# Four modulation chunks moved into the last step of a recurrent mixer, and half of an output product for four token tiles taken from raw weights

## The chip, the cores and the metric

The kernel runs on one core of a Trainium2 chip. The metric is the device time of one execution in microseconds. Engines are named as in the profile: PE is TensorE, DVE is VectorE, ACT is ScalarE, POOL is GpSimd, and SP is the queue that issues nearly all transfers.

## The reference, cut to what matters

The network has two layers for 512 latent tokens and 256 context tokens of width 1024. Only the first mixer of layer 0, a bidirectional gated recurrence, and the modulation vectors are touched.

```
m  = silu(c) @ ada_w + ada_b                     # 6 vectors of 1024 for each layer
u  = conv(px[..., D_RNN:]);  px = h @ w_in       # D_RNN = 1280 = 10 blocks of 128
a, b = coeffs(u, w_a, w_x, lambda)               # two gates per block and direction
hs = scan_forward(a, b) + scan_backward(a, b)
yx = (gelu(px[..., :D_RNN]) * hs) @ w_out        # the output product
x  = x + gt1 * yx
```

The modulation vectors of layer 1 (shift and scale of its first norm) are read only some 600 us after the stretch in which they are made here.

## The kernel before, in words

**The mixer's steps.** The ten blocks are worked in five pairs by `step(s)`, s = 0 to 5. Step s projects pair s (`stage_a`) and finishes pair s-1: the gates (`gates`, PE products into PSUM tiles `pg`, L623), the gated GELU branch (`stage_c`, PE products into `pa`, L415 and L416, and a GELU on ACT, L666), and the scans on DVE (`scans`). Step 5, the last, has no projection. For each of its two blocks and two directions ACT computes `tr`, `ti`, `q`, `a` (L631 to L638), DVE combines them (L640, L641, L643), and ACT turns `a` into the decay (L642). We call this sequence a gate group; there are four of them in the step, c0 forward, c0 backward, c1 forward, c1 backward. After the fourth come four square roots on ACT (L648), the last two GELUs, and the last scans, whose product with the GELU (L663) completes rows of `yrg`, the mixer's output y, transposed. The tiles `ti`, `q` and `a` have one buffer each, so a gate group of step 5 waits until the scans of step 4 have read theirs.

**The modulation chunks.** `ada(l, n)` makes 256 columns of a modulation vector: a 1 MB load into the pool `ws` (3 buffers, shared with `w_in` and `w_out`), 16 PE products (L176) into a `pg` tile, a copy to `part` on ACT (L178), and for every second chunk four small PE products (L185) into another `pg` tile and one or two additions on DVE (L188, L192). `pg` has two buffers, shared with the gates. There are 24 chunks, five in a step and four in step 4.

**The output product.** `mix_out` multiplies y (10 chunks of 128 rows) with `w_out` in two halves of 512 columns, for six token tiles. The rule is three PE products of split operands for each chunk: high times high, high times low, low times high (L808), where weights are split by ACT (`wohi`, L306) and POOL (`wolo`, L309), and y by ACT and DVE (`yt` for chunks 0 to 7, `yb` for 8 and 9). For the first half and the first four token tiles, chunks listed in `early` use the unsplit fp32 operands in one product (L804). `NEARLY[0]` is the number of such chunks. The first four tiles accumulate in PSUM tiles `po`, the other two in `pt`.

**What sets the order.** Outside regions marked as manual, the build step schedules each engine's queue from the code by costs of its own. Step 5 is manual for ACT alone, so ACT runs it as written there, and the other engines' order comes from that scheduler. Each engine then works its queue strictly in that order. The tiles of `mix_out` lie in memory that the mixer frees: `yt` and the routing tables wait for the last product of `stage_c`, the split weights for the last scans.

Of the kernel before, what the change touches and what calls it, by code (L numbers as in the profile page):

```python
# [17 lines left out]
P = 128  # L18
# [19 lines left out]
NPAIR = NE // 2  # L38
NWIDE = 6
FIRST = 5  # L40
NEARLY = 6, 4
KWB = 5
BIG = 1.0e30

# [58 lines left out]
class Net:  # L103
# [285 lines left out]
    def rg_mixer(self, ctx_y, wsp):  # L389
        tc, nc, A = self.tc, self.nc, self.A  # L390
        self.y = ctx_y.tile([P, NB, NTOK], F32, name="yrg")
        with ExitStack() as st:
# [35 lines left out]
            with tc.tile_pool(name="n0", bufs=1) as wk, tc.tile_pool(name="p0", bufs=2, space=PSUM) as p0:  # L428
# [18 lines left out]
                with tc.manual_schedule(engines={ET.PE, ET.DVE, ET.Activation, ET.Pool}):  # L447
# [7 lines left out]
                    rows = {}  # L455
# [93 lines left out]
                    parts = [split(uw[0], c, nc.gpsimd if c else nc.vector, wk, c) for c in range(2)]  # L549
# [34 lines left out]
            pb = st.enter_context(tc.tile_pool(name="pb", bufs=2, space=PSUM))  # L584
            ada = [(0, n) for n in range(8, 24)] + [(1, n) for n in range(8)]
            with tc.tile_pool(name="ma", bufs=2) as wa, tc.tile_pool(name="m0", bufs=2) as wk, \
# [27 lines left out]
                def gates(s, parts, c):  # L614
                    b = 2 * s + c
                    u = uc[b]
                    uh, ul, gh, gl = parts

                    def gate(m):
                        ps = pb.tile([P, 1024], F32, name="pg")  # L620
                        for j, (g, v) in enumerate(((gh, uh), (gh, ul), (gl, uh))):
                            for o, z in ((CTX, NTOK), (0, CTX)):
                                nc.tensor.matmul(ps[:, 256 + o:256 + z], g[:, m, :], v[:, o:z],  # L623
                                                 start=j == 0, stop=j == 2)
                        return ps[:, 256:1024]

                    for d in range(2):
                        v = d * NB + b
                        ps = gate(2 * d)
                        tr = wk.tile([P, NTOK], F32, name="tr", bufs=1)  # L630
                        nc.scalar.activation(tr, ps, AF.Tanh, scale=0.5, bias=self.ba[:, v:v + 1])  # L631
                        ps = gate(2 * d + 1)
                        ti = w1.tile([P, NTOK], F32, name=f"ti{2 * c + d}")
                        nc.scalar.activation(ti, ps, AF.Tanh, scale=0.5, bias=self.bx[:, v:v + 1])
                        q = w1.tile([P, NTOK], F32, name=f"q{2 * c + d}")
                        nc.scalar.activation(q, tr, AF.Exp, scale=self.cl[:, 0, v:v + 1], bias=self.cl[:, 0, v:v + 1])
                        a = w1.tile([P, NTOK], F32, name=f"a{2 * c + d}")
                        nc.scalar.activation(a, tr, AF.Tanh, scale=self.cl[:, 1, v:v + 1], bias=self.cl[:, 1, v:v + 1])  # L638

                        nc.vector.scalar_tensor_tensor(a, q, 1.0, a, op0=OP.add, op1=OP.mult)  # L640
                        nc.vector.scalar_tensor_tensor(q, a, 2.0, a, op0=OP.add, op1=OP.mult)  # L641
                        nc.scalar.activation(a, a, AF.Identity, bias=self.ones)  # L642
                        nc.vector.scalar_tensor_tensor(ti, ti, 1.0, u, op0=OP.add, op1=OP.mult)  # L643
                        yield c, d, q, a, ti
# [31 lines left out]
                NS = NB // 2  # L676
                wg = {}

                def step(s):
                    ps = []  # L680
                    if s < NS:
                        wg[s] = load_gates(s)
                        stage_a(s, uw[s])
                    if s >= 1:
                        wc = load(256 * (s - 1))
                        gp = [gate_parts(s - 1, wg[s - 1], c) for c in range(2)]
                        for c in range(2):
                            ps += gates(s - 1, gp[c], c)
                        if s == NS:
                            roots(ps)  # L690
                        for c in range(2):
                            stage_c(s - 1, wc, c)
                    if 0 < s < NS - 1:
                        uw.append(load(DR + 256 * (s + 1)))
                    for l, n in ada[s * 5:s * 5 + 5]:
                        self.ada(l, n, wsp, pb, wk)
                    if s >= 1:
                        if s < NS:
                            roots(ps)
                        scans(s - 1, ps)  # L700
# [6 lines left out]
    def mix_out(self, l, x, NT, y, K, W, rt, wsp, ypool, ytp, ring, nring):  # L707


        tc, nc, A = self.tc, self.nc, self.A  # L710
        V = nc.vector
# [4 lines left out]
        with ExitStack() as st:  # L716
# [5 lines left out]
            order = list(range(K)) if l == 0 else [0, 2, 4, 6, 1, 3, 5, 7]  # L722
# [9 lines left out]
            def parts(h, raw, i, ks):  # L732
                hi = wop.tile([P, 2, 512], F32R, name="wohi")
                lo = wop.tile([P, 2, 512], F32R, name="wolo")
                self.split(hi, lo, raw[:, ks, :], V if l and h == 0 and i else nc.gpsimd)
                for j, k in enumerate(range(4)[ks]):
                    wo[h, i + k] = hi[:, j, :], lo[:, j, :]
# [3 lines left out]
            if K > 8:  # L741
                yb = w1.tile([P, 2, K - 8, NT * P], F32R, name="yb")

            def rows(t, ks):
                self.split(yt[t][:, 0, ks], yt[t][:, 1, ks], y[:, ks, t * P:(t + 1) * P], V)

            raws = {i: load(0, i) for i in range(0, K, 4)}
            early = {k: (y[:, k, :], raws[k - k % 4][:, k % 4, :]) for k in order[0:NEARLY[l]]}
            if l == 0:
                parts(0, raws[4], 4, slice(2, 4))  # L750
                parts(0, raws[8], 8, slice(0, 2))
                for t in range(4):
                    rows(t, slice(6, 8))
                self.split(yb[:, 0], yb[:, 1], y[:, 8:, :], V)
                for i, j in ((0, 0), (0, 2), (4, 0)):
                    parts(0, raws[i], i, slice(j, j + 2))
                for t in range(4, NT):
                    rows(t, slice(0, 8))
                for t in range(4):
                    rows(t, slice(0, 6))  # L760
            else:
                for i in (0, 4):
                    parts(0, raws[i], i, slice(1, 4, 2))
                for a in (1, 0):
                    for t in range(NT):
                        rows(t, slice(a, 8, 2))
# [11 lines left out]
            wk = st.enter_context(tc.tile_pool(name="ro2", bufs=2, side="right"))  # L778
# [13 lines left out]
            for n, a, b in (("grp", 0, NG), ("exp", 8, NR)):  # L792
                s = A[f"l{l}_moe_b_{n}"]
# [7 lines left out]
            def mm(ps, h, k, t):  # L801
                if h == 0 and t < 4 and k in early:
                    a, b = early[k]
                    nc.tensor.matmul(ps, a[:, t * P:(t + 1) * P], b, start=k == order[0], stop=False)  # L804
                    return
                (yh, yl), (wh, wl) = ys(k, t), wo[h, k]
                for j, (a, b) in enumerate(((yh, wh), (yh, wl), (yl, wh))):
                    nc.tensor.matmul(ps, a, b, start=k == order[0] and j == 0,  # L808
                                     stop=k == order[-1] and j == 2)
# [1364 lines left out]
```

## Time and profile before

| What | Value |
|---|---|
| runs shown | 1882.44, 1895.56, 1926.79 us (median 1895.56) |
| the profiled execution's own time | 1883.95 us |
| its span, first to last instruction | 1881.9 us |
| mean granted TensorE clock | 0.963 |
| PE busy | 1742.4 us, 93% |
| DVE, ACT, POOL busy | 948.0, 543.5, 384.1 us |
| HBM read | 518.59 MB, 279 GB/s over the span |

A busy PE is not PE at its peak. The granted clock is given as a fraction of 2.4 GHz, so 0.50 is 1.2 GHz. A number in square brackets at the end of a timeline row is the time that the engine stood idle before it, and what ended that.

### The profile page before, as it was taken

To read this page: it belongs to the slowest core of one execution; us is meant where nothing else is said; L and a number is where in the kernel's file an instruction comes from. 1 tells how busy PE (TensorE), PEld (TensorE's weight loads), DVE (VectorE), ACT (ScalarE), POOL (GpSimd) and SP (SyncE) were. 2 spreads that over 40 slices of the span, in tenths; PEclk is the share of its full clock that TensorE was granted. 3 is DMA by queue.
4 is the path that set the end of the run, shared out by engine and by line. 5 is a ranking of instruction groups with operands and counts; after the bars stand their busy time and mean duration, and the time that the engine had idled before them with its cause. 6 is when DMAs were issued, how large, how long until landed. Compare 5 with 4: busy or idle time off the path is not lost. (4 is left out here: it accounts for less than half of the span.)

```text
span 1881.9 us, 26126 instructions
## 1 busy us (share of the span) xinstructions
PE 1742.4 (93%) x10181; PEld 1041.3 (55%) x10181; DVE 948.0 (50%) x1879; ACT 543.5 (29%) x1007; POOL 384.1 (20%) x300
## 2 busy tenths in 40 slices
PE   7999998997999999999989999999969999999996
PEld 5777776684443434344437898876733434433342
DVE  5477776656545464555465744255642333333233
ACT  5367775432101111111126312236321111111112
POOL 3433322401111010101034333211211111011111
PEclk9999998998999999999999999999988999999998
DMA  9544432556999989999942545101869999999996
GB/s 331 176 156 150 127 122 91 179 173 233 418 419 419 386 323 419 419 419 418 418 165 83 164 157 179 46 1 39 301 277 398 422 421 420 421 421 420 421 421 246
DMA packets 158244, 527.75 MB, mean 280 GB/s; under 512 B 15132, under 2 KB 92194, under 8 KB 109988
## 3 DMA queue, kind: packets, MB, share of 16 engines
q1 hardware_dynamic: 151348, 497.09, 68.1%
q0 software_dynamic: 6768, 28.93, 3.9%
q8 instruction: 82, 1.34, 0.3%
q14 instruction: 46, 0.38, 0.1%
HBM read 518.59 MB, written 7.39 MB: 279 GB/s over the span
## 5 line engine op out<-in xcount | busy, mean ns | idle before, releaser
L1215 DVE TENSOR_TENSOR xl<-xl,ps 128x512 f32<-128x512 f32 x136 | 87.7, 683 | 302.4 <-PE ps L1213 302.4
L1200 POOL DMA_INDIRECT xg<-h_rows,idx x32 | 36.7, 1146 | 582.7 <-DVE slot L1185 249.1
L1277 PE MATMUL pd<-wring,hT 128*64 128x512 f32 (+1 forms) x616 | 152.2, 610 | 2.7 <-ACT hT L1269 2.1
L1252 PE MATMUL pu<-wring,xT 128*64 128x512 f32 (+1 forms) x576 | 149.9, 610 | 2.0 <-DMA wring<-in_l_moe_w_up_dram 2.0
L309 POOL TENSOR_TENSOR wlo<-ws,whi 128x1024 fp32r<-128x1024 f32 x41 | 112.9, 2762 | 117.5 <-ACT whi L306 103.4
L1240 POOL TENSOR_TENSOR yl<-yw,yh 128x512 fp32r<-128x512 f32 x60 | 76.6, 1277 | 252.3 <-ACT yh L1239 250.2
L1252 PE MATMUL pg<-wring,xT 128*64 128x512 f32 (+1 forms) x576 | 127.7, 594 | 0.0
L1259 ACT ACTIVATE sg<-pg 128x512 f32<-128x512 f32 x32 | 19.1, 597 | 355.3 <-PE pg L1252 355.3
L1689 PE MATMUL pa<-whi,hhi 128*128 128x256 f32 x352 | 104.0, 295 | 10.4 <-ACT v L1786 5.1
L1239 ACT ACTIVATE yh<-yw 128x512 fp32r<-128x512 f32 x64 | 40.3, 630 | 251.5 <-DVE yw L1236 127.7
L1231 DVE SCALAR_TENSOR_TENSOR yw<-pd,slotr,gt2b 128x512 f32<-128x512 f32 x62 | 46.5, 751 | 120.2 <-PE pd L1277 120.2
L1689 PE MATMUL pa<-whi,hlo 128*128 128x256 f32 x352 | 102.7, 292 | 0.0
L1689 PE MATMUL pa<-wlo,hhi 128*128 128x256 f32 x352 | 102.3, 291 | 0.0
L1252 PE MATMUL pu<-yt,xT 128*64 128x512 f32 (+1 forms) x408 | 95.6, 596 | 0.3 <-DMA yt<-in_l_moe_w_up_dram 0.3
L1277 PE MATMUL pd<-yt,hT 128*64 128x512 f32 (+1 forms) x376 | 87.6, 599 | 1.6 <-ACT hT L1269 1.1
L1208 ACT ACTIVATE xT<-tr 128x512 f32<-128x512 f32 x64 | 35.1, 595 | 185.2 <-PE tr L1207 185.2
L1277 PEld LDWEIGHTS pd<-wring,hT 128*64 128x64 f32 (+1 forms) x616 | 44.4, 133 | 75.1 <-issue 69.2
L1252 PEld LDWEIGHTS pu<-wring,xT 128*64 128x64 f32 (+1 forms) x576 | 40.9, 132 | 76.7 <-issue 68.5
L1215 DVE TENSOR_TENSOR xl<-xl,pd 128x512 f32<-128x512 f32 x128 | 82.1, 680 | 0.5 <-PE pd L1213 0.5
L1252 PE MATMUL pg<-yt,xT 128*64 128x512 f32 (+1 forms) x400 | 81.4, 596 | 0.0
L1213 PE MATMUL ps<-yh,oht 128*128 128x512 f32 x166 | 75.4, 454 | 5.9 <-DVEq L1356 5.9
L1252 PEld LDWEIGHTS pg<-wring,xT 128*64 128x64 f32 (+1 forms) x576 | 38.5, 131 | 70.9 <-issue 68.6
(627 smaller groups left out, 3935.1 us busy)
## 6 DMA issues: line engine op xcount, KB each, us to landing
wring<-in_l_moe_w_gate_dram SPq DMA_DIRECT2D x62, 1024.0 KB
wring<-in_l_moe_w_up_dram SPq DMA_DIRECT2D x61, 1024.0 KB
wring<-in_l_moe_w_down_dram SPq DMA_DIRECT2D x59, 1024.0 KB
yt<-in_l_moe_w_up_dram SPq DMA_DIRECT2D x41, 1024.0 KB
ws<-in_l_ada_w_dram SPq DMA_DIRECT2D x40, 1024.0 KB
yt<-in_l_moe_w_gate_dram SPq DMA_DIRECT2D x39, 1024.0 KB
yt<-in_l_moe_w_down_dram SPq DMA_DIRECT2D x35, 1024.0 KB
ws<-in_l_moe_w_gate_dram SPq DMA_DIRECT2D x24, 1024.0 KB
```

Of the source, the lines that this page charges most:

```text
L309: eng_lo.tensor_sub(lo, x, hi.bitcast(F32))
L1200: nc.gpsimd.indirect_dma_start(out=xg, out_offset=None, in_=hd, in_offset=bass.IndirectOffsetOnAxis(ap=idx[:, 0:1], axis=0))
L1208: nc.scalar.activation(xT[:, 4 * h:4 * h + 4, :], pt[:, :, 0:n], AF.Copy)
L1213: nc.tensor.matmul(ps, lhsT, y, start=i == 0, stop=i == len(ys) - 1)
L1215: V.tensor_add(xs, xs, ps)
L1231: V.scalar_tensor_tensor(y[k], ps, r[:, 1:2], g[:, 0, :], op0=OP.mult, op1=OP.mult)
L1239: nc.scalar.activation(yh, y, AF.Copy)
L1240: eng.tensor_sub(yl, y, yh.bitcast(F32))
L1252: nc.tensor.matmul(ps[a:a + w, :], xT[:, 4 * h + j, a:a + w], pieces[n, e[i], h][:, j, :], start=h == 0 and j == 0, stop=h == 1 and j == 3)
L1259: nc.scalar.activation(s, pg, AF.Silu)
L1277: nc.tensor.matmul(pd[a:a + w, :], hT[:, 2 * h + j, a:a + w], ring.down(2 * p + i, h, j, c), start=h == 0 and j == 0, stop=h == 1 and j == 1)
L1689: nc.tensor.matmul(ps, h, w[:, k % 4, :], start=k == 0 and j == 0, stop=k == KD - 1 and j == 2)
```

## The change

Three edits. `NEARLY[0]` goes from 6 to 10, so all ten chunks of the first half are raw for the first four token tiles, and the last raw product closes the accumulation. The splits of `mix_out` are written in another order: weights from chunk 0 on, then `yt` of tiles 4 and 5, then `yb`, then `yt` of tiles 0 to 3 in one piece each. The four chunks of step 4 (layer 1, n = 4 to 7) move to step 5: two after the gate groups of c0, two after those of c1.

```diff
-NEARLY = 6, 4
+NEARLY = 10, 4
...
                         for c in range(2):
                             ps += gates(s - 1, gp[c], c)
+                            if s == NS:
+                                for l, n in ada[20 + 2 * c:22 + 2 * c]:
+                                    self.ada(l, n, wsp, pb, wk)
...
-                    for l, n in ada[s * 5:s * 5 + 5]:
+                    for l, n in ada[s * 5:s * 5 + 5] if s < 4 else ():
                         self.ada(l, n, wsp, pb, wk)
...
             if l == 0:
-                parts(0, raws[4], 4, slice(2, 4))
-                parts(0, raws[8], 8, slice(0, 2))
-                for t in range(4):
-                    rows(t, slice(6, 8))
-                self.split(yb[:, 0], yb[:, 1], y[:, 8:, :], V)
-                for i, j in ((0, 0), (0, 2), (4, 0)):
-                    parts(0, raws[i], i, slice(j, j + 2))
+                for i in range(0, K, 2):
+                    parts(0, raws[i - i % 4], i - i % 4, slice(i % 4, i % 4 + 2))
                 for t in range(4, NT):
                     rows(t, slice(0, 8))
+                self.split(yb[:, 0], yb[:, 1], y[:, 8:, :], V)
                 for t in range(4):
-                    rows(t, slice(0, 6))
+                    rows(t, slice(0, 8))
...
-                    nc.tensor.matmul(ps, a[:, t * P:(t + 1) * P], b, start=k == order[0], stop=False)
+                    nc.tensor.matmul(ps, a[:, t * P:(t + 1) * P], b, start=k == order[0], stop=k == order[-1])
```

Three places show how the queues move. The first is SP around the loads of step 4 and 5, as a difference (`rg_w_in` is the weight of `stage_c`, `ada_w` a modulation chunk, `rg_w_out` a raw third of the output weight).

```order
 L168 DMA ws<-in_l_ada_w_dram 128x8x256
-L401 DMA ws<-in_l_rg_w_in_dram 128x8x256
+L401 DMA ws<-in_l_rg_w_in_dram 128x8x256 x2
 L168 DMA ws<-in_l_ada_w_dram 128x8x256 x4
-L401 DMA ws<-in_l_rg_w_in_dram 128x8x256
-L728 DMA ws<-in_l_rg_w_out_dram 128x4x512 x2
```

The weight of the last `stage_c` is now loaded ahead of the four chunks, not behind them, and the raw output weights stand behind chunks that are consumed in step 5.

The second place is ACT in step 5, from the decay of the second gate group to that of the fourth. Before:

```order
L642 ACTIVATE a_2581<-a_2581,ones 128x768
L631 ACTIVATE tr<-pg,hb 128x768
L634 ACTIVATE ti_2603<-pg,hb 128x768
L636 ACTIVATE q_2605<-tr,cl 128x768
L638 ACTIVATE a_2607<-tr,cl 128x768
L642 ACTIVATE a_2607<-a_2607,ones 128x768
```

And with the change:

```order
L642 ACTIVATE a_2517<-a_2517,ones 128x768
L178 ACTIVATE part<-pg 128x256 x2
L631 ACTIVATE tr<-pg,hb 128x768
L634 ACTIVATE ti_2571<-pg,hb 128x768
L636 ACTIVATE q_2573<-tr,cl 128x768
L638 ACTIVATE a_2575<-tr,cl 128x768
L306 ACTIVATE yt<-yrg 128x1024 x4
L642 ACTIVATE a_2575<-a_2575,ones 128x768
```

DVE in the same place, with the change, around the decay of the second group:

```order
L640 SCALAR_TENSOR_TENSOR a1_2517<-q1_2515,a1_2517 128x768
L965 MEMSET cum2_2800 128x1
L970 TENSOR_SCALAR tb_2802<-pidx_84 128x6
L641 SCALAR_TENSOR_TENSOR q1_2515<-a1_2517 128x768
L188 TENSOR_TENSOR modT_78<-pg_2548,svm1_136 128x2x4
```

Two copies of the modulation stand between the second and the third group, and four splits of y ahead of the third decay. Two more splits stand ahead of the fourth decay, where before six stood (four of 256 columns, two of 1024), and two more copies behind it. On DVE the two small writes of `mix_out` (L965, L970; before they stood ahead of the fourth group) wait for the last product of `stage_c` and stand inside the second group.

The third place is PE around the gates of block c1, with the change. First the end of `stage_c`, ahead of the third gate group:

```order
L415 MATMUL pa<-hhi,wlo 128x512
L416 MATMUL pa<-hhi,wlo 128x256
L415 MATMUL pa<-hlo,whi 128x512
L416 MATMUL pa<-hlo,whi 128x256
L185 MATMUL pg<-sel,part 128x2 x4
L623 MATMUL pg<-uh,gh 128x512
```

Then, behind the last gate product of the step:

```order
L623 MATMUL pg<-ul,gh 128x256
L623 MATMUL pg<-uh,glo 128x512
L623 MATMUL pg<-uh,glo 128x256
L176 MATMUL pg<-ws,cT 32x256 x16
L185 MATMUL pg<-sel,part 128x2 x4
L803 MATMUL po<-ws,yrg 128x512 x40
```

The products of `stage_c` (`pa`) are all done before the gates of c1, which stand back to back, and the 40 raw products stand behind the last modulation sums. Before, `pa` products stood between all gate groups, and the 24 raw products stood directly behind the last of the `pa`:

```order
L416 MATMUL pa<-hhi,wlo 128x256
L415 MATMUL pa<-hlo,whi 128x512
L416 MATMUL pa<-hlo,whi 128x256
L804 MATMUL po<-ws,yrg 128x512 x24
L808 MATMUL po<-wohi,yt 128x512 x4
```

## Rows read from the trace of the kernel before

**Rows 1.** The page's head, and the granted clock in 40 slices.

```profile
span 1881.9 us, 26126 instructions
...
PEclk9999998998999999999999999999988999999998
```

**Rows 2.** PE, from the timeline: start, length, line, operands, count, idle before.

```profile
274.62 1.93 PE L176 MATMUL pg<-ws,cT 128*32 128x256 f32 x32
...
279.45 1.26 PE L185 MATMUL pg<-sel,part 128*128 128x2 f32 x8 [2.90 <-ACT part L178]
280.64 3.35 PE L176 MATMUL pg<-ws,cT 128*32 128x256 f32 x32
...
308.31 1.01 PE L623 MATMUL pg<-uh,gh 128*128 128x512 f32 x2 [3.29 <-ACT tr L631]
309.11 0.84 PE L623 MATMUL pg<-ul,gh 128*128 128x512 f32 x2
...
324.16 20.76 PE L804 MATMUL po<-ws,yrg 128*128 128x512 f32 x48
348.31 1.99 PE L808 MATMUL po<-wohi,yt 128*128 128x512 f32 x4 [3.38 <-ACT wohi L306]
...
362.95 0.39 PE L808 MATMUL pt<-wohi,yt 128*128 128x512 f32 x1
```

**Rows 3.** ACT, from the timeline, steps 4 and 5.

```profile
279.04 0.64 ACT L178 ACTIVATE part<-pg 128x256 f32<-128x256 f32 x2
...
282.70 0.38 ACT L178 ACTIVATE part<-pg 128x256 f32<-128x256 f32 x1 [0.87 <-PE pg L176]
284.07 0.38 ACT L178 ACTIVATE part<-pg 128x256 f32<-128x256 f32 x1 [0.98 <-PE pg L176]
...
306.53 0.93 ACT L642 ACTIVATE a<-a,ones 128x768 f32<-128x768 f32 x1 [8.94 <-DVE q L641]
...
312.89 0.94 ACT L642 ACTIVATE a<-a,ones 128x768 f32<-128x768 f32 x1 [2.02 <-DVE q L641]
...
324.42 3.23 ACT L306 ACTIVATE yt<-yrg 128x256 fp32r<-128x256 f32 x6 [0.81 <-PE pa L416]
327.56 0.92 ACT L642 ACTIVATE a<-a,ones 128x768 f32<-128x768 f32 x1
```

**Rows 4.** DVE, from the timeline.

```profile
214.77 2.83 DVE L640 SCALAR_TENSOR_TENSOR a<-q,a 128x768 f32<-128x768 f32 x1 [1.33 <-ACT a L638]
...
276.21 0.96 DVE L640 SCALAR_TENSOR_TENSOR a<-q,a 128x768 f32<-128x768 f32 x1 [5.07 <-ACT a L638]
...
288.99 3.86 DVE L654 TENSOR_TENSOR_SCAN ti<-a,q 128x768 f32<-128x768 f32 x1
...
296.38 3.14 DVE L663 TENSOR_TENSOR yrg<-yrg,ti 128x768 f32<-128x768 f32 x1
...
310.90 0.96 DVE L640 SCALAR_TENSOR_TENSOR a<-q,a 128x768 f32<-128x768 f32 x1 [0.87 <-ACT a L638]
...
324.37 0.35 DVE L971 TENSOR_SCALAR tb<-pidx 128x6 bf16<-128x6 f32 x1 [5.15 <-issue]
...
332.40 1.75 DVE L654 TENSOR_TENSOR_SCAN ti<-a,q 128x768 f32<-128x768 f32 x1
```

**Rows 5.** POOL, from the timeline.

```profile
214.37 2.42 POOL L309 TENSOR_TENSOR wlo<-ws,whi 128x1024 fp32r<-128x1024 f32 x1
...
284.08 1.05 POOL L308 TENSOR_SCALAR whi<-ws 128x1024 fp32r<-128x1024 f32 x1 [32.81 <-PE pg L176]
```

**Rows 6.** Busy time of each engine in stretches, then granted clock, DMA share, GB/s.

```profile
306.00:324.00 18.00, 15.70 (x74) 13.64 (x75) 6.25 (x7) 13.04 (x15) 0.00 (x0) 0.81 0.00 1
...
348.00:356.00 8.00, 7.22 (x18) 5.21 (x19) 2.67 (x2) 5.42 (x6) 7.67 (x3) 0.57 0.41 138
```

**Rows 7.** Groups by line, 286 to 330 us: operands, count, busy us, mean ns.

```profile
L306 ACT ACTIVATE yt<-yrg 128x1024 fp32r<-128x1024 f32 x2 | 2.0, 1040 | 0.0
...
L309 DVE TENSOR_TENSOR yt<-yrg,yt 128x1024 fp32r<-128x1024 f32 x2 | 2.4, 1216 | 0.0
```

## The prediction

> **What bounds the kernel now.** The page's head [rows 1] gives a span of 1881.9 us, and its clock row shows TensorE near its full clock nearly everywhere. The profiled execution's own time is 1883.95 us, so 2.05 us lie around the span. That run is 11.6 us below the median of the three shown (1895.56) and 1.5 us above the lowest (1882.44); the sum below is made against it.
>
> The chain of waits says little here, so I read the timelines of the engines between 274 and 363 us, the only stretch whose queues the change reorders. I then asked what the first product into `pt` (tiles 4 and 5) waits for: behind it both programs have the same order on every engine, with only two small exceptions in PE's tail, so its shift is the shift of the end. It starts at 362.95 [rows 2]. Ahead of it three things take turns. From 284 to 306 us DVE is the bound: it finishes the scans of step 4 while POOL works beside it. From 306 to 324 us ACT and DVE pass the gate groups to and fro, one each 312.89 - 306.53 = 6.36 us, of which ACT stands idle 2.02 [rows 3], while PE is covered by `stage_c`. From 324.16 PE is the bound: 24 raw products in 20.76 us, 0.865 us each, then 3.38 us of idling for the first split weight, then 48 products that begin at the lower clock: 0.57 over eight microseconds [rows 2, 6].
>
> **The sum, part by part.**
>
> *Removed from step 4.* The four chunks' copies stood on ACT ahead of the square roots: 0.64 + 0.38 + 0.38 us of work and 0.87 + 0.98 us of waiting for their products [rows 3]: -3.2 us. The products themselves (1.93 us for two chunks at full clock, 3.35 at the lower one [rows 2]) leave a place where PE waited anyway, and cost nothing there. The loads leave too: the weight of the last `stage_c` no longer queues behind them. POOL waited 32.81 us for it, for a buffer that a chunk held, and split it from 284.08 on [rows 5]. Now POOL splits each block as soon as step 4's products free the tiles.
>
> *What that moves.* The second of these splits now falls at about 275 to 278 us, beside the last L640 of step 4, which took 0.96 us alone [rows 4]. The nearest row is one step earlier, where the same split (214.37, 2.42 us [rows 5]) held the same DVE operation: 2.83 us at 214.77 [rows 4]. So +1.9 on the chain. In exchange the splits no longer stand beside the scans. A scan took 3.86 us there against 1.75 alone; the product at 296.38 took 3.14 against 0.96 [rows 4]: -4.3 us from those two. Together the first decay of step 5 moves by -3.2 + 1.9 - 4.3 = -5.6, from 306.53 to 300.9. Bounds: -3.5 if the gate splits of POOL, which stay, meet the scans more often, and -7.5 if all the slowed scans recover.
>
> *Added to step 5, first pair.* Between the second and third group ACT now copies two parts and PE sums them; before, the copies began at 279.04 and the sums ended with 279.45 + 1.26 [rows 2, 3]: 1.6 us. The third group's gates must follow, because they share the two `pg` buffers. Three pairs of products make a gate, 0.84 to 1.01 us a pair at the lower clock [rows 2]; overlapping they take about 2.1, half of that at full clock. Before, these gates were done ahead of ACT. I take 1.6 + 2.1 = 3.7 us; bounds 2.6 (full clock) and 5.0 (the second gate late as well). The two chunks' products lie on PE beside the second group.
>
> *Splits of y inside the gate groups.* ACT has four splits of 1.04 us [rows 7] ahead of the third decay, in the gap of 2.02 us: they pipeline to 3.7, so +1.7. In the fourth group DVE has a split of 1.22 us [rows 7] ahead of its last operation: +1.1. Before, six splits (3.23 us) and the small write at 324.37, which had waited for PE [rows 3, 4], delayed the fourth decay from the regular 325.61 to 327.56.
>
> So the fourth decay starts at 300.9 + 3 x 6.36 + 3.7 + 1.7 + 1.1 = 326.5, 1.1 us earlier than before.
>
> *From there to the raw products.* Before, they did not wait for this decay: PE had them at 324.16. Now the second pair's sums stand ahead of them in PE's queue, and their PSUM tiles lie where `pg` was. After the decay (0.92) come copies and sums (1.6) and an addition on DVE (some 0.3, of the size of the small write at 324.37 [rows 4]): 2.8 us. The raw products start at 329.3.
>
> *Raw products.* 40 at 0.865 = 34.6 us. They replace 24 such products and 48 split ones, whose stretch was 348.31 to 362.95 [rows 2]. The last scans and the weight splits run under them: the last rows of y are needed at 329.3 + 32 x 0.865 = 357, and before, the scans and the first weight split were through 348.31 - 327.56 = 20.8 us after the fourth decay [rows 2, 3], which is 347 now. The idle 3.38 us vanish.
>
> *Clock.* PE has nothing from the last chunk's products to 329.3, about 5 us. The one comparable row: after 3.38 us of idling the clock was 0.57 over 8 us [rows 2, 6], which is 8 x 0.43 = 3.4 us lost. I add 3.4; bounds 0 and 3.4 + 1. The page "TensorE: Matmul & The Clock Gate" of the Trainium skill (Part 1: The HAM clock gate) says that this ramp costs under 1% of a typical kernel's span and is not to be fitted to a count; by that the term would be left out and the sum would end at +1.0. The row decides, since the whole effect here is of that size.
>
> The first `pt` product then starts at 329.3 + 34.6 + 3.4 = 367.3, against 362.95: +4.4. What stands behind it keeps its distance, since the second half's loads wait for the raw products and its splits for `pt`. **1883.95 + 4.4 = 1888.3, say 1888 us.** With all bounds favourable it is 1.9 + 1.1 + 3.4 = 6.4 us less (1882), with all adverse 2.1 + 1.3 + 1.0 = 4.4 more (1893).
>
> **The rivals.**
>
> *First, the gain stays (chance 0.2).* If the first decay comes 7.5 us earlier and PE keeps its clock through the short bursts of c1, the boundary costs 2.6 and the raw products run at 0.865 from the start: the favourable end, 1882 us. For it: the clock does not fall at once. Against: the stretch with the shortest bursts, 306 to 324, stood at 0.81 [rows 6], and the idle time ahead of the raw products is now longer than the 3.38 us.
>
> *Second, slower, PE holds DVE in the second gate group (chance 0.2).* The two small DVE writes wait for the last product of `stage_c`, and now stand ahead of the second group's last operation. Most of the second block's products and two chunks must be done by the end of that group's L640, which before started 310.90 - 306.53 = 4.4 us behind the first decay [rows 3, 4] and took 0.96: 306.2. These products can run from about 294, when the first group's `ti` has been read, and at full clock I estimate 10 us for them, so 304. At the lower clock, to which PE fell after the idle wait at 308.31 [rows 2], they need some 6 us more, and from 306.2 on each microsecond delays ACT by as much: +4.5 at most, 1893 us. The same page's section on HAM oscillation describes this pattern, bursts between waits that stay throttled; the clock of 0.81 here agrees with it, and no run yet shows it for the new order.
>
> *Third, no change at all (0.05):* that the scheduler hides all of it is spoken against by the orders shown; 1884 us.
>
> The likeliest, as summed, has 0.55.
>
> **The numbers.** 2% of 1884 us is 37.7 us, about what a measurement of this kernel can tell from no change, since the runs shown lie up to 44 us apart. No case comes near it: within 2% has 0.97. The change would have to lose 38 us in a stretch of 88 us; I leave 0.01 for faster and 0.02 for slower, the latter for runs like the slowest one shown. The cases alone span 1882 to 1893. The median of a few runs lay above the profiled one before, so the range goes from 1878 to 1903; the likeliest case's own range is 1884 to 1893.
>
> **What would show it.** Right: POOL's last `wlo` splits end before 280 us; the first decay of step 5 starts near 301 and the fourth near 326.5; the raw block starts about 2.8 us after that, at a clock near 0.5, and lasts 38 us; no idle time stands between raw and split products; the first `pt` product starts near 367.3. Wrong: the third group's `tr` follows its copies within 1.5 us; raw products run at 0.865 us from the first; the small DVE writes wait for PE in the second group; or anything shifts behind that by another amount than `pt`. A raw block that waits for its weights on a load would refute the cover that I assume for SP's new order.

## The result and the profile after

The changed kernel took 1893.64 us (median of 20 executions, 1881.43 to 1930.0), the kernel before 1885.05 us (20 executions, 1875.3 to 1926.79). Ratios leave out executions more than 1.5% above the fastest of the same kernel, here 4 of the 20 and 5 of the 20. The ratio is 1.0051, 95% interval 1.0027 to 1.0075: 9.6 us slower (5.1 to 14.1), where I had forecast 4.4. The profiled execution took 1899.1 us, with a span of 1897.1 us at a mean granted clock of 0.956; PE was busy 1755.6 us in it, 13 more than before.

Ahead of step 5, on POOL and DVE (timeline; columns as in [rows 2]):

```profile
268.23 2.39 POOL L309 TENSOR_TENSOR wlo<-ws,whi 128x1024 fp32r<-128x1024 f32 x1
...
276.31 2.40 POOL L309 TENSOR_TENSOR wlo<-ws,whi 128x1024 fp32r<-128x1024 f32 x1
```

```profile
277.43 2.10 DVE L640 SCALAR_TENSOR_TENSOR a<-q,a 128x768 f32<-128x768 f32 x1 [4.26 <-ACT a L638]
...
286.02 2.78 DVE L654 TENSOR_TENSOR_SCAN ti<-a,q 128x768 f32<-128x768 f32 x1
...
293.19 0.93 DVE L663 TENSOR_TENSOR yrg<-yrg,ti 128x768 f32<-128x768 f32 x1
...
304.94 0.17 DVE L970 TENSOR_SCALAR tb<-pidx 128x6 bf16<-128x6 f32 x1
```

These answer [rows 4, 5]. The second split ends before 280 us, beside an L640 that takes 2.10 us, where it took 0.96. The first split stands beside an earlier L640, which takes 2.80 us at 268.63 (0.96 at 268.44 before). The scan that took 3.86 us takes 2.78 and the product that took 3.14 takes 0.93. The last row is one of the two small writes: no idle time stands before it.

ACT in step 5 (timeline), the rows that answer to [rows 3]:

```profile
299.67 0.94 ACT L642 ACTIVATE a<-a,ones 128x768 f32<-128x768 f32 x1 [4.17 <-DVE q L641]
...
306.04 0.93 ACT L642 ACTIVATE a<-a,ones 128x768 f32<-128x768 f32 x1 [2.02 <-DVE q L641]
306.88 0.64 ACT L178 ACTIVATE part<-pg 128x256 f32<-128x256 f32 x2
311.33 0.90 ACT L631 ACTIVATE tr<-pg,hb 128x768 f32<-128x768 f32 x1 [3.82 <-PE pg L623]
313.19 0.90 ACT L634 ACTIVATE ti<-pg,hb 128x768 f32<-128x768 f32 x1 [0.96 <-PE pg L623]
...
315.89 3.90 ACT L306 ACTIVATE yt<-yrg 128x1024 fp32r<-128x1024 f32 x4
319.69 0.92 ACT L642 ACTIVATE a<-a,ones 128x768 f32<-128x768 f32 x1
...
327.13 0.93 ACT L642 ACTIVATE a<-a,ones 128x768 f32<-128x768 f32 x1 [1.22 <-DVE q L641]
```

The decays stand 6.37, 13.65 and 7.44 us apart. The middle distance holds the boundary: copies at 306.88, the third group's `tr` only at 311.33, and `ti` late as well.

PE (timeline), the rows that answer to [rows 2], and below them the clock (busy time by engine, then granted clock, DMA share, GB/s), the answer to [rows 6]:

```profile
307.30 1.81 PE L185 MATMUL pg<-sel,part 128*128 128x2 f32 x8 [3.01 <-ACT part L178]
308.97 0.99 PE L623 MATMUL pg<-uh,gh 128*128 128x512 f32 x2
...
321.45 3.39 PE L176 MATMUL pg<-ws,cT 128*32 128x256 f32 x32 [5.66 <-ACT tr L631]
...
328.39 1.87 PE L185 MATMUL pg<-sel,part 128*128 128x2 f32 x8 [3.55 <-ACT part L178]
330.51 36.66 PE L803 MATMUL po<-ws,yrg 128*128 128x512 f32 x80 [0.26 <-DVE modT L188]
366.61 0.79 PE L807 MATMUL pt<-wohi,yt 128*128 128x512 f32 x1
```

```profile
306.00:324.00 18.00, 11.05 (x56) 8.46 (x60) 8.62 (x11) 13.19 (x17) 0.00 (x0) 0.73 0.67 257
...
330.00:334.00 4.00, 3.74 (x6) 1.68 (x6) 3.54 (x5) 3.98 (x5) 0.00 (x0) 0.50 0.00 0
334.00:338.00 4.00, 4.00 (x10) 1.84 (x9) 4.00 (x5) 1.77 (x3) 0.00 (x0) 0.91 0.00 0
```

The raw block waits for the second pair's sums, starts at half the clock, and nothing idles between it and the first `pt` product, which starts 3.66 us later than in [rows 2]. Up to here the sum is nearly met. But this pair of executions lies 15 us apart. By the distance of equal ACT instructions some 3 us of it are there from the end of layer 0's mixer up to 1060 us, and at 1300 us it is 16, in layer 1's mixer, whose code is untouched. Most of the growth falls between 1260 and 1300 us. These are stretches of 20 us, in the changed kernel and then in the kernel before:

```profile
1260.00:1280.00 20.00, 20.00 (x102) 14.26 (x102) 10.41 (x32) 9.39 (x32) 1.27 (x1) 0.83 0.00 1
1280.00:1300.00 20.00, 20.00 (x101) 14.38 (x101) 11.15 (x34) 12.59 (x43) 2.49 (x2) 0.84 0.01 1
1300.00:1320.00 20.00, 20.00 (x89) 14.31 (x89) 9.26 (x27) 9.44 (x35) 3.76 (x3) 0.81 0.00 0
```

```profile
1260.00:1280.00 20.00, 20.00 (x114) 14.37 (x114) 11.14 (x34) 12.37 (x43) 2.50 (x2) 1.00 0.01 2
1280.00:1300.00 20.00, 20.00 (x112) 14.23 (x112) 11.97 (x38) 11.83 (x46) 2.49 (x2) 1.00 0.00 0
1300.00:1320.00 20.00, 20.00 (x77) 11.39 (x76) 11.71 (x28) 11.61 (x37) 3.89 (x7) 1.00 0.38 132
```

PE is busy for all of every stretch. What differs ahead of everything else is the granted clock: 20 x (0.17 + 0.16 + 0.19) = 10.4 us are lost. I call this a spell.

### The profile page after: what moved, and what is told of

It is laid out like the page before. It is cut to its first block, busy times and chain, and to the rows that moved or that the text cites. A ratio compares the mean times of both kernels' runs of the same rounds, so it can differ in the third digit from the quotient of the medians.

```text
span 1897.1 us, 26088 instructions
## 1 busy us (share of the span) xinstructions
PE 1755.6 (93%) x10165; PEld 1045.4 (55%) x10165; DVE 947.7 (50%) x1875; ACT 543.5 (29%) x1003; POOL 383.6 (20%) x300
## 5 line engine op out<-in xcount | busy, mean ns | idle before, releaser
L1688 PE MATMUL pa<-whi,hlo 128*128 128x256 f32 x352 | 104.2, 296 | 0.0
L1688 PEld LDWEIGHTS pa<-whi,hhi 128*128 128x128 f32 x352 | 71.9, 204 | 12.4 <-ACT v L1785 8.4
```

The source lines that it names most:

```text
L1688: nc.tensor.matmul(ps, h, w[:, k % 4, :], start=k == 0 and j == 0, stop=k == KD - 1 and j == 2)
```

## Theories

**Local:** the change costs what the first `pt` product shows, about 3 us, less or more by what the router behind it makes of it; the rest of the 9.6 is spells that any kernel has. **Downstream:** the change itself draws spells into layer 1. **Dear raws:** the 16 added raw products are the cost. Behind the first half of the output product comes the router, which picks an expert for each token: DVE adds the products to `xc` and `xl` and makes the router's weights `gw`, PE transposes the sums (`pt<-ident,xc`), and ACT copies them to `h2T`, one copy after another. Because executions differ by some us at their start, places below are measured in us from the first decay of step 4 (258.74 us in [rows 2]'s execution) in the same trace.

| kernel | raw start | first `pt` | first `h2T` copy | last `h2T` copy of layer 0 |
|---|---|---|---|---|
| before, null, null2 | 65.4, 65.8, 64.3 | 104.2, 104.2, 102.7 | 119.3, 119.3, 117.8 | 182.0, 183.7, 182.1 |
| changed, again, again2, again3 | 71.6, 71.4, 70.0, 70.3 | 107.7, 107.4, 106.2, 107.3 | 124.5, 124.2, 123.1, 124.1 | 184.9, 184.6, 183.4, 188.2 |
| chunks_only | 70.6 | 104.5 | 119.6 | 183.9 |
| raw_only | 65.7 | 99.6 | 119.7 | 184.0 |
| front_only | 60.7 | 100.9 | 116.0 | 180.3 |
| front_raw, front_raw2 | 60.7, 62.5 | 96.9, 98.1 | 113.7, 115.0 | 174.0, 175.4 |

## Experiment 1: both kernels again

No edit. The changed kernel three times, the kernel before twice, beside 118 more executions of the kernel before in the batches of all experiments.

> The changed kernel once more, nothing edited. Local theory (the change adds 3.7 us in the stretch that it touches and nothing behind it): the first product on pt (L807) again 3 to 5 us later than in the kernel before, the distance then stays between +2 and +6 us up to the end wherever the granted clock of both is the same, ratio 1.001 to 1.004. Downstream theory (the later start of layer 0's product upsets layer 1's mixer, where the profiled pair drifted from +3 to +15 us): the distance grows again by 8 us or more in layer 1's mixer, at the same place, and the ratio is 1.005 to 1.008.

> The changed kernel a third time, nothing edited, for a third trace and more executions. Local theory: measured from the first decay of step 4 (L642), the first product on pt comes 107.5 us later (107.68 and 107.36 so far; 104.2 in both traces of the kernel before) and the first product of the router 127 us later (122.9 before); what lies between the granted clock's low spells adds nothing behind that. Spell theory: a stretch of some 20 us at half the clock while TensorE is busy throughout, as in layer 1's mixer in both traces so far (10.2 and 12.0 us lost), stands in this trace too, and 4 to 7 of 12 executions have a mean granted clock under 0.962, where the kernel before has 3 to 5.

> The changed kernel a fourth time, nothing edited, since its ratio was 1.0051, 1.0032 and 1.0011 so far. Local theory (3 us at the first product on pt, of which the router's stretch gives 1.5 to 2 back by a clock that stays up, and no more behind it): executions with a mean granted clock of 0.962 and over stand 2 to 5 us above those of the kernel before, ratio 1.001 to 1.004. Spell theory (this kernel draws low spells of TensorE's clock into layer 1's mixer more often than the kernel before): 6 or more of 12 executions under 0.962, the kernel before in the same batch at a third or less, and again a spell of some 10 us in the trace.

> The kernel before once more, nothing edited: ratio 1.000 within 0.003 under every theory. Its trace is a second one of the kernel before. Local theory: the first product on pt (L807 there L808) at 362 to 364 us again, and the low clock in layer 1's mixer (1260 to 1320 us, granted clock 1.00 in the first trace of before and 0.81 to 0.84 in that of the changed kernel) comes and goes between executions of one kernel. Downstream theory: 1.00 there again, as it belongs to the kernel before.

> The kernel before a third time. Local theory: spells in layer 1's mixer belong to every kernel, and come or stay away by execution; if this trace shows one (as one execution in three should, by 36 of 102 executions under a mean clock of 0.962), it is a stretch of 10 us or more lost with TensorE busy throughout. Spell theory: none, as in its two traces so far.

The changed kernel's ratio was 1.0032 (1.0005 to 1.0059), 1.0011 (0.9980 to 1.0042) and 1.0029 (0.9995 to 1.0063); the unchanged one's 1.0005 (0.9982 to 1.0029) and 1.0028 (0.9986 to 1.0071). Each execution's mean granted clock orders its time: at 0.962 and over, the changed kernel took 1883.2 us (mean of 25 of its 56 executions), the kernel before 1878.5 us (89 of 142), a difference of 4.7 +- 1.5 us (95%); batch by batch it is 5.8, 3.5 and 3.6. This sorts executions by a part of their outcome, so it describes and does not prove. At 0.955 to 0.961 the changed kernel stands some 12 us higher, below that 22 to 47 us. The first `pt` product of null came at 359.53 us and not at 362 to 364 as I expected, but its first decay of step 4 stood 3.45 us earlier too.

Between 1260 and 1320 us all four traces of the changed kernel have spells that lose 10 to 12 us. One of the three of the kernel before has one as well, a smaller one; null2:

```profile
1260.00:1280.00 20.00, 20.00 (x91) 14.41 (x90) 7.86 (x28) 9.62 (x31) 2.49 (x2) 0.74 0.00 1
```

That is 5.2 us lost, against my expectation that it would be 10 or nothing. Spells belong to both kernels. That they come more often in the changed one (31 of 56 executions under 0.962, against 53 of 142) is likely but not shown: in the batches of 31 and more executions of the kernel before, that share itself went from 31% to 48%. So the downstream theory stands open.

## Experiment 2: each part alone

chunks_only keeps the old splits and 24 raw products; raw_only leaves the chunks in step 4. The 40 raw products and the new order of the splits were not tried apart.

```diff
 # chunks_only
+                            if s == NS:
+                                for l, n in ada[20 + 2 * c:22 + 2 * c]:
+                                    self.ada(l, n, wsp, pb, wk)
...
-                    for l, n in ada[s * 5:s * 5 + 5]:
+                    for l, n in ada[s * 5:s * 5 + 5] if s < 4 else ():
 # raw_only
-NEARLY = 6, 4
+NEARLY = 10, 4
 ...
```

> The kernel before with the four chunks moved to step 5 alone; the four token tiles keep 24 raw products and 16 x 3 from splits. Local theory: first decay near 300 us, boundary behind the gates of 3 to 4.5 us, raws start near 330 us instead of 324.2, and since the wait of the split products for y's split (to 363 us before) covers most of that, the first product on pt at 363 to 366 us: 0 to +3 us, ratio 1.000 to 1.002. Theory of the dear raws (the 16 added raw products are the cost): first product on pt as before, ratio 1.000 or just under. Downstream theory: as local in the trace, and +8 us or more by the end.

> The kernel before with the raw products and the order of the splits alone; the chunks stay in step 4. Local theory: raws start at 324 us as before, 40 of 0.865 us take them to 358.8 us, or 360 to 361 us with the clock's loss of 1.5 to 2 us that the changed kernel showed, and the first product on pt follows at once: 2 to 4 us earlier than 362.95, ratio 0.998 to 0.999. Theory of the dear raws: first product on pt at 363 us or later, ratio 1.000 to 1.005. Downstream theory (any move of this point upsets layer 1): a ratio other than the local shift by 8 us or more.

Ratios: 1.0008 (0.9983 to 1.0032) and 0.9991 (0.9958 to 1.0024), neither told apart from no change. The traces tell more. chunks_only starts its raws 5.5 us later than the mean of the three traces of before, yet its first `pt` product only 0.8 us later; on PE:

```profile
326.11 23.14 PE L807 MATMUL po<-ws,yrg 128*128 128x512 f32 x48 [0.26 <-DVE modT L188]
...
348.68 0.80 PE L811 MATMUL po<-wohi,yt 128*128 128x512 f32 x1
```

```profile
348.00:356.00 8.00, 8.00 (x34) 6.10 (x33) 0.91 (x1) 0.00 (x0) 7.31 (x6) 1.00 0.61 202
```

The idle 3.38 us of [rows 2] behind the 24 raw products are gone: the weight splits, for which PE waited there, are ready by then. With the wait goes the low clock behind it, 0.57 in [rows 6] and 1.00 here, some 3.4 us; the raws themselves lose 1.8 us (22.6 us up to the first product from splits, against 20.8). That slack, 3.4 + 3.4 - 1.8 = 5.0 us, hid nearly all of the later start. raw_only removes the same slack from the other side and its first `pt` product comes 4.1 us earlier:

```profile
323.78 34.50 PE L800 MATMUL po<-ws,yrg 128*128 128x512 f32 x80
357.71 0.79 PE L804 MATMUL pt<-wohi,yt 128*128 128x512 f32 x1
...
376.64 1.12 PE L851 MATMUL pt<-ident,xc 128*128 128x128 f32 x4 [4.02 <-DVE tmp L809]
```

So 40 raws cost 34 us and are not dear up to this point; that theory falls. Alone, the two parts move the first `pt` product by +0.8 and -4.1 us, together by +3.4: they spend one slack twice. But raw_only keeps nothing: its first `h2T` copy is 0.9 us late and its last 1.4. The last row shows where: PE idles 4.02 us for DVE. DVE's rows in raw_only, and then in null:

```profile
360.52 4.71 DVE L811 TENSOR_TENSOR xc<-xc,tmp 128x512 f32<-128x512 f32 x2
...
366.35 4.51 DVE L811 TENSOR_TENSOR xl<-xl,tmp 128x512 f32<-128x512 f32 x2
370.78 5.20 DVE L834 TENSOR_TENSOR gw<-wr,modT 128x320 f32<-128x320 f32 x2
```

```profile
358.98 1.28 DVE L815 TENSOR_TENSOR xc<-xc,tmp 128x512 f32<-128x512 f32 x2
...
361.37 1.28 DVE L815 TENSOR_TENSOR xl<-xl,tmp 128x512 f32<-128x512 f32 x2
...
364.47 2.31 DVE L838 TENSOR_TENSOR gw<-wr,modT 128x320 f32<-128x320 f32 x2 [1.81 <-DMA wr<-in_l_moe_w_exp_dram]
```

The same three pairs take 14.4 us instead of 4.9. In raw_only POOL splits weights during 14.64 of the 16 us from 360 on. The page "SBUF — State Buffer" of the Trainium skill (section "SBUF: two separate sides") says that an operation of VectorE with two SBUF inputs and one of GpSimd that reads SBUF shut each other out for a whole instruction; these rows agree with it, with 4.71 us beside the splits against 1.28. The changed kernel pays there too, less:

```profile
371.82 5.10 DVE L814 TENSOR_TENSOR xl<-xl,tmp 128x512 f32<-128x512 f32 x2
```

From the first `pt` product to the first `h2T` copy pass 15.1 us in all five traces with the old order of the splits and nothing added, 16.8 in all six traces that have the new order with the chunks in step 5, and 20.1 in raw_only. In raw_only the clock is low behind the idle 4.02 us as well:

```profile
372.00:376.00 4.00, 0.62 (x16) 0.54 (x15) 4.00 (x3) 1.06 (x1) 3.59 (x2) 0.81 1.03 424
376.00:380.00 4.00, 3.36 (x10) 2.57 (x10) 2.61 (x6) 1.21 (x3) 0.00 (x0) 0.50 1.01 426
```

In layer 1's mixer, between 1260 and 1320 us, neither part's trace has a spell, and 2 of 12 executions of each stand under 0.962, where in that batch the changed kernel has 7 of 12 and the kernel before 13 of 35. That fits the downstream theory without showing it.

## Experiment 3: a pure delay

Products that change nothing, ahead of the first one on `pt`, in the kernel before; 16 of them, then 32.

```diff
+                if l == 0 and t0 == 4:
+                    for t in range(16):
+                        nc.tensor.matmul(ps[0], ys(order[0], 4)[0], wo[0, order[0]][0], start=True, stop=True)
                 for k in order:
```

> The kernel before with 16 products of 128x512 from splits added ahead of the first product on pt, which they don't change (the first real product starts the sum anew): 16 x 0.227 = 3.6 us, so that the first product on pt stands where the changed kernel has it (+3.3 to +3.7 us) with nothing else changed. Theory that a delay there passes on whole: +3.6 us in all, ratio 1.002. Theory that it is partly hidden: the second product of the router +1 us or less and ratio 1.000 to 1.001. Downstream theory (a later layer 0 brings low spells into layer 1): a spell of 10 us in layer 1's mixer and ratio 1.003 to 1.006.

> The kernel before with 32 added products of 128x512 from splits ahead of the first product on pt, twice the earlier delay: 32 x 0.227 = 7.3 us. Theory that a delay passes on whole: in the trace +7 us at the first product of the router (130 us behind the first decay of step 4, 122.9 in the kernel before), and executions with a mean clock of 0.962 and over at 1884 to 1887 us, ratio 1.003 to 1.005. Theory of a spared clock (a busier TensorE ahead of the router gives some of it back): +4 to +6 us. Spell theory (a later layer 1 draws low spells): 6 or more of 12 executions under 0.962 and the kernel before in the same batch at a third; if the two shares are alike, a later start alone doesn't draw them.

Ratios: 0.9995 (0.9956 to 1.0035) and 1.0026 (1.0000 to 1.0053). By the last `h2T` copy the 3.6 us cost 4.6 (187.1) and the 7.3 us only 3.3 (185.9), against 182.6. At a clock of 0.962 and over, the 32 products cost 7.1 +- 2.2 us (1885.5 against 1878.4 in their batch), the 16 cost 1.9 +- 5. So at the last `h2T` copy a delay can be worth some 3 us less than its length. The profiled executions of both have spells in layer 1 of about 29 us, and under 0.962 were 7 of 13 and 4 of 13 executions (11 of 35 and 4 of 17 in the kernel before beside them). That does not show that a later start draws spells, nor that it does not.

The place that decides is the router's entry on PE. Its waits before, then in the changed kernel, then in delay32:

```profile
381.02 0.63 PE L839 MATMUL pl<-ident,cT 40*128 40x40 f32 x4 [1.62 <-DVE cT L835]
```

```profile
382.77 0.66 PE L854 MATMUL pt<-ident,xc 128*128 128x128 f32 x4 [1.25 <-DVE tmp L812]
...
385.69 0.63 PE L838 MATMUL pl<-ident,cT 40*128 40x40 f32 x4 [0.86 <-DVE cT L834]
```

```profile
383.44 0.63 PE L842 MATMUL pl<-ident,cT 40*128 40x40 f32 x4 [1.62 <-DVE cT L838]
```

The clock there, in the same three:

```profile
379.00:381.00 2.00, 0.40 (x2) 0.00 (x0) 2.00 (x3) 0.25 (x2) 1.35 (x1) 1.00 0.85 344
381.00:383.00 2.00, 1.98 (x13) 1.87 (x14) 0.27 (x2) 0.00 (x0) 0.00 (x0) 0.89 0.97 348
383.00:385.00 2.00, 2.00 (x6) 1.58 (x5) 0.00 (x0) 0.00 (x0) 0.00 (x0) 0.50 0.74 303
```

```profile
384.00:386.00 2.00, 1.14 (x7) 0.66 (x5) 1.70 (x4) 0.67 (x3) 0.42 (x1) 1.00 1.11 438
386.00:388.00 2.00, 2.00 (x15) 1.82 (x15) 0.24 (x1) 0.00 (x0) 0.00 (x0) 1.00 0.88 369
```

```profile
385.00:387.00 2.00, 2.00 (x11) 1.61 (x11) 0.00 (x0) 0.00 (x0) 0.00 (x0) 1.00 0.92 389
```

Before, one wait of 1.62 us is followed by 0.50; in the changed kernel two shorter waits are not, and it wins 2.3 us or more back: the first two `h2T` copies stand 6.3 us apart in it, 8.6 to 9.8 in the three traces of before. Neither holds always. In again3 the clock fell to 0.50 for some 10 us, and its last `h2T` copy is 3.3 us and more behind those of the other three. In delay32 the same 1.62 us were not followed by the low clock (7.0 us between the copies), which is where its 7.3 us shrank, but for 1.3 us by which it stood early ahead of the added products (102.4 against 103.7); in delay they were (10.0 us). From the first to the last copy pass 60.4 to 61.2 us where the clock stayed up and 62.7 to 64.3 where it fell.

## Experiment 4: the chunks ahead of the gates

The boundary exists because the chunks stand between two gate groups that share `pg` with them. At the head of step 5, where ACT waits for DVE anyway, they should hold up less. front_raw has all else of the change (its edit, against the changed kernel, is shown), front_only the old splits and 24 raw products.

```diff
+                        if s == NS:
+                            for l, n in ada[20:24]:
+                                self.ada(l, n, wsp, pb, wk)
                         for c in range(2):
                             ps += gates(s - 1, gp[c], c)
-                            if s == NS:
-                                for l, n in ada[20 + 2 * c:22 + 2 * c]:
-                                    self.ada(l, n, wsp, pb, wk)
```

> The changed kernel with its four chunks at the head of step 5, ahead of both gate groups, in place of behind each. Local theory: no boundary behind the second gate group (4.45 us in the changed kernel), the fourth decay of step 5 comes 6 us or more earlier than in the kernel before, raws start 58 to 60 us behind the first decay of step 4 (71.5 in the changed kernel, 65.6 in the kernel before), the first product on pt at 93 to 96 us (107.5 and 104.2): 8 to 11 us earlier than in the kernel before, ratio 0.994 to 0.997 if the router follows. Rival: the router doesn't follow, since VectorE's sums and GpSimd's splits of the second half fall together, as in the kernel with the raw products alone, whose 4.6 us were gone at the router: ratio 0.998 to 1.001. Second rival: TensorE waits at the head of step 5 for the chunks' weights and the gain is lost there: first decay not earlier than 47 us.

> The kernel before with the four chunks at the head of step 5, and its own splits (24 raw products). Local theory: raws start at 58 to 60 us behind the first decay of step 4; the products from splits behind them wait for ScalarE's splits of wohi (3.4 us of wait in the kernel before), which come as much earlier as the fourth decay: first product on pt at 94 to 98 us, ratio 0.994 to 0.998. Rival (the boundary is only moved): first decay at 47 us or later, first product on pt at 102 to 106 us, ratio 0.999 to 1.002.

> The version with the chunks at the head of step 5 once more: ratio 0.992 to 0.997 if its 0.9941 holds. If 0.9941 came from executions that the clock happened to spare: 0.997 to 1.000.

front_raw against the kernel before: 0.9941 (0.9912 to 0.9969), and again 0.9974 (0.9942 to 1.0007). At a clock of 0.962 and over it took 1870.5 us (13 of 24 executions), 8.0 +- 2.0 us less than the kernel before, and its last `h2T` copy is 7.9 us earlier. The second comparison alone does not tell it from no change; taken together this version beats the kernel before. It beats the changed kernel too: beside it in the same two batches that took 1881.9 and 1882.3 us at that clock, this version 1870.6 and 1870.5. The gain on the way was smaller than I expected: its first `pt` product came 6.9 and 5.6 us earlier than in the kernel before (not 8 to 11), its fourth decay 2.6 and 0.7 (not 6 or more). As in the changed kernel the router then cost 1.7 us more, and the clock stayed up behind it in both traces. front_only: 0.9976 (0.9945 to 1.0008), its first `pt` product later than I expected (100.9, not 94 to 98), as PE still waited 2.50 and 1.93 us for the first split weights; its gain is 2.3 us at the last `h2T` copy. ACT and PE in front_raw:

```profile
303.27 0.94 ACT L642 ACTIVATE a<-a,ones 128x768 f32<-128x768 f32 x1 [2.02 <-DVE q L641]
...
309.64 0.94 ACT L642 ACTIVATE a<-a,ones 128x768 f32<-128x768 f32 x1 [2.02 <-DVE q L641]
...
316.01 0.94 ACT L642 ACTIVATE a<-a,ones 128x768 f32<-128x768 f32 x1 [0.22 <-DVE q L641]
```

```profile
318.57 36.73 PE L803 MATMUL po<-ws,yrg 128*128 128x512 f32 x80 [3.94 <-ACT ti L634]
354.74 0.79 PE L807 MATMUL pt<-wohi,yt 128*128 128x512 f32 x1
```

The three decays are 6.37 us apart: no boundary. The first comes 45.4 us behind the first decay of step 4, 4.6 later than in the changed kernel's first trace (46.9 and 6.2 later in front_raw2), as the chunks now stand ahead of the first gate group. The raws no longer wait for the fourth decay, and start 11 us earlier than in the changed kernel's first trace.

## Why the prediction was right or wrong

**The step that failed** is the last of the sum: "behind it both programs have the same order [...] so its shift is the shift of the end", and with it "What stands behind it keeps its distance". The shift at the first `pt` product was right in sign and size: +3.4 us by four traces of the changed kernel and three of before, against +4.4. What comes behind did not keep its distance, though its order is the same; this was also the prediction's own sign of being wrong. At the first `h2T` copy the shift is +5.2, as DVE's sums and `gw` fall beside POOL's splits there and take 1.7 us more. At the last copy it is +2.7 (+0.9 to +5.6 by trace), as in three traces of four the clock stays up where it falls in the kernel before. Spells in layer 1's mixer, for which the sum had no term, then added 10 to 12 us to each profiled execution of the changed kernel and 0, 0 and 5 to those of the kernel before. The whole is +4.7 +- 1.5 us where the mean clock was 0.962 and over; some 2 us of that lie behind the last `h2T` copy, and no run tells where. In the first comparison the means of the 16 and 15 executions in the ratio differ by 7.7 us: 5.0 between their lower groups (up to 1889.54 and 1885.59, 7 and 11 executions), the rest from the share of the higher ones (9 of 16 from 1892.31 on, 4 of 15 from 1892.13 on). The ratio's 9.6 stands 2 us above that, inside its interval. Three repeats gave 2 to 6 us. So the +4.4 was too small for the first comparison, and about right for executions of like clock, by luck: what the router adds and gives back, and the 2 us behind it, were not in the sum. Of the theories, the dear raws fall at the first `pt` product, the local one accounts for the +2.7, and the downstream one stays open, as does the cause of the spells.

**The base failed too.** 1888 was made against one profiled execution (1883.95). Beside the median then shown it read as 7.6 us faster, though every term said slower. The kernel before came to 1885.05 over 20 executions; 4.4 more is 1889.5, and the changed kernel's median was 4.2 above that.

The terms, in the first trace of each kernel:

- First decay: -5.6 forecast, -7.1 measured (299.67, in an execution that stood 0.2 us later by then); over the three and four traces it is -7.7, past my bound of -7.5. The last L640 lost 1.1, not 1.9, but the first split held an earlier one as well, and the fourth decay of step 4 came 2.2 us later (280.56 against 278.20, less those 0.2). The recovery of the scans was right in kind and larger than forecast.
- Second to third decay: 3.7 for the boundary and 1.7 for four splits forecast, 13.65 - 6.36 = 7.3 measured. `tr` was 4.45 us behind the copies, and `ti` waited 0.96 more: the second gate was late as well, the case of my upper bound. In again, again2 and again3 the decays stand 13.6, 12.1 and 12.5 us apart.
- Third to fourth: +1.1 forecast, 7.44 - 6.36 = 1.1 measured.
- Fourth decay to raws: 2.8 forecast, 3.4 measured.
- Raws and clock: 38.0 forecast, 36.1 measured: 34.6 of work and 1.5 of clock loss, not 3.4. In the traces behind it this stretch took 36.0, 36.2 and 37.0 us.

The errors, -1.5, +1.9, 0.0, +0.6 and -1.9 us, nearly cancel, so that the shift at the first `pt` product came out closer than its terms.

**The rivals.** The first (the gain stays) is false: boundary and low clock came as feared. The second (PE holds DVE in the second gate group) is false: 304.94 shows no wait. Its price was also summed wrongly: 304 + 6 - 306.2 gives 3.8 us, not 4.5. The third is false.

**The two rules on the clock.** Of the page "TensorE: Matmul & The Clock Gate" of the Trainium skill (Part 1: The HAM clock gate) the rule that the ramp is under 1% of a span and not to be fitted would have left the clock term out, and the row put it at 3.4 us; 1.5 us measured lies between the two. The rule is on the ramp alone: over the whole span the clock fell short by 69 us in null and 83 us in the changed kernel's first trace, 3.7% and 4.4%, and no run tells ramps from the rest. The pattern of its section on HAM oscillation, a wait between bursts and then the low clock, agrees with 372 to 380 us of raw_only; the spells of layer 1 have no wait that the busy time shows, and no run here tells their cause.

## What to carry to other kernels

Ask of a moved piece of work what shares its buffers: two small chunks cost some 4 to 5 us between two gate groups, and all four 4.6 to 6.2 us ahead of both, where they no longer hold up what follows. When two edits each look free, look whether they are paid from the same idle time. And follow a shift beyond the last reordered instruction, to the next wait at which engines meet again, before calling it the shift of the end.

## What the runs showed of the hardware

- With PE busy throughout, its granted clock fell to 0.50 for stretches of 10 to 60 us in layer 1's mixer: 0.52 over 1300 to 1320 us in again, and under 0.55 for 60 us in delay32. I had expected low clocks only behind idle time. The places agree to a few us between changed and again3, and between again and again2.
- At the router's entry one wait of 1.62 us was followed by the low clock in six traces of seven (not in delay32); two of 1.25 and 0.86 us close together were not in five of six (in again3 it fell behind the first).
- Two sums on DVE took 1.28 us alone and up to 5.10 beside POOL's splits.
